# Rolling a large matrix by DMA: the long row pieces copied in 16 DMAs of whole pieces, or in 512 DMAs of half pieces

## The chip, the cores and the metric

One core of a Trainium2 chip runs the kernel; the other cores do nothing. The metric is the device time of one execution in microseconds (us). The kernel before took 818.08 us, the median of 11 runs that lie between 815.44 and 820.29 us.

## What is computed

The reference is a circular shift of every row:

```
x = np.random.randn(8192, 8192).astype(np.float32)
shift = 100
return np.roll(x, shift, axis=1)
```

Nothing is calculated. Each output row is the input row moved 100 columns to the right, and the last 100 columns of the input come first. 268.44 MB are read from the chip's memory and 268.44 MB are written to it.

## The kernel before

The kernel splits every output row in two at column a = 128, the shift rounded up to a multiple of 128 columns (512 bytes). The long piece, columns 128 to 8191 (32,256 bytes), is copied from memory to memory without touching the on-chip memory. The short head, columns 0 to 127 (512 bytes), takes another way. The source of the long piece begins at column g = 28, which is byte 112 of the row.

**The long pieces** (lines 30 to 37). A row number is written as 64c + 4e + j, with c from 0 to 127, e from 0 to 15 and j from 0 to 3. The views `xm` and `om` (lines 30 and 31) put j first, then e, then c. Line 37 issues one DMA for each of 4 blocks of c and each of 4 values of j: 16 DMAs. The outermost dimension of a DMA is e with 16 values, so that each of the core's 16 DMA engines gets the rows of one e; within a DMA an engine has `depth` = 32 rows, one for each c of the block. One DMA moves 16 x 32 rows, 16,128 KB. An even j goes to the queue of SyncE (SP) and an odd j to that of ScalarE (ACT):

```
engines[j % 2].dma_start(out=om[j, :, cs, a:], in_=xm[j, :, cs, g:n_cols - s])
```

So each of the two queues issues 8 DMAs. In the profile the DMA ring that SP feeds is q1 and the one that ACT feeds is q10. SP and ACT do nothing else in this kernel.

**The heads** (lines 54 to 76). GpSimd (POOL) issues them on a queue of its own (ring q0): in two stages k it reads the pieces for 4096 rows each into on-chip tiles `t` and `h` (lines 67, 68 and 71), VectorE copies parts of `t` into `h` (lines 69 and 72), and at the end POOL issues 8 DMAs that write `h` to the output (line 76). The heads are 8.39 MB of the traffic on the rings. Nothing on SP or ACT depends on them.

**What sets the order.** The program is written in a framework that places the waits itself. It gives each DMA a completion semaphore out of a small set and uses them in turn. The trace shows eight of them on SP and ACT, four on each queue. The fifth DMA of a queue therefore waits until the first one has landed on all 16 engines, the sixth waits for the second, and so on: at most four DMAs of a queue are in flight. No DMA of the long pieces waits for anything else.

Of the kernel before, what the change touches and what calls it, by code (L numbers as in the profile page):

```python
# [1 line left out]

# [4 lines left out]


@with_exitstack
def kernel(  # L10
    ctx: ExitStack,
    tc: tile.TileContext,
    x: bass.AP,
    shift: int,
    out: bass.AP,
):
    nc = tc.nc
    n_rows, n_cols = x.shape
    s = shift % n_cols
    a = -(-s // 128) * 128  # L20
    g = a - s
    P = nc.NUM_PARTITIONS
    engines = [nc.sync, nc.scalar]
    n_chunks = 16
    rows = n_rows // n_chunks

    xm = x.rearrange("(c e j) w -> j e c w", e=16, j=4)  # L30
    om = out.rearrange("(c e j) w -> j e c w", e=16, j=4)
    depth = n_rows // 64 // 4
    for c in range(4):
        for j in range(4):
            if a < n_cols:
                cs = slice(c * depth, (c + 1) * depth)
                engines[j % 2].dma_start(out=om[j, :, cs, a:], in_=xm[j, :, cs, g:n_cols - s])
    if a == 0:
        return


    if a > 512:
        for i in range(n_chunks):
            r = slice(i * rows, (i + 1) * rows)
            nc.gpsimd.dma_start(out=out[r, :s], in_=x[r, n_cols - s:])
            if g > 0:
                nc.gpsimd.dma_start(out=out[r, s:a], in_=x[r, :g])
        return

    Q, J = 4, 8
    n_st = n_rows // (P * Q * J)
    reads = ctx.enter_context(tc.tile_pool(name="reads", bufs=n_st))
    heads = ctx.enter_context(tc.tile_pool(name="heads", bufs=n_st))
    xt = x.rearrange("(k p j q) c -> k q p j c", q=Q, j=J, p=P)
    ot = out.rearrange("(k p j q) c -> k q p j c", q=Q, j=J, p=P)
    tiles = []  # L60
    for k in range(n_st):
        t = reads.tile([P, Q - 1, J, a], x.dtype)
        h = heads.tile([P, Q, J, a], x.dtype)
        for q in range(1, Q):
            lead = bass.AP(tensor=x.tensor, offset=(k * P * J * Q + q) * n_cols - s,
                           ap=[[J * Q * n_cols, P], [Q * n_cols, J], [1, a]])
            nc.gpsimd.dma_start(out=t[:, q - 1], in_=lead)  # L67
        nc.gpsimd.dma_start(out=h[:, Q - 1, :, :s], in_=xt[k, Q - 1, :, :, n_cols - s:])  # L68
        nc.vector.tensor_copy(h[:, :Q - 1, :, :s], t[:, :, :, :s])  # L69
        if g > 0:  # L70
            nc.gpsimd.dma_start(out=h[:, 0, :, s:], in_=xt[k, 0, :, :, :g])  # L71
            nc.vector.tensor_copy(h[:, 1:, :, s:], t[:, :, :, s:])  # L72
        tiles.append(h)
    for k, h in enumerate(tiles):
        for q in range(Q):
            nc.gpsimd.dma_start(out=ot[k, q, :, :, :a], in_=h[:, q])  # L76


# [1 line left out]
_INS = ['x', 'shift']  # L80
_OUTS = [((8192, 8192), 'float32')]

_NUMBERS = {'shift': 100}


# [26 lines left out]
```

## Time and profile before

| | us |
|---|---|
| median of 11 runs | 818.08 |
| lowest and highest | 815.44 and 820.29 |
| the profiled execution's own time | 817.92 |
| its span, first to last instruction | 816.1 |
| VectorE busy | 3.7 |
| GpSimd busy | 16.1 |
| issue to landing, long pieces, median, SP and ACT | 399.4 and 398.3 |

The span is what the profile's views cover; the other 1.8 us of the profiled execution lie around it. A "packet" in the profile is one contiguous run of bytes that one DMA engine moves, or the 4-byte write with which that engine reports the end of its part of a DMA. The "share of 16 engines" of a ring is the time its packets took, divided by 16 engines times the span. "GB/s" counts each byte once, as it passes through a DMA engine; a copy from memory to memory loads the memory twice for it, once as a read and once as a write.

### The profile page before, as it was taken

What the parts mean: (1) busy time and instruction counts of PE and PEld (TensorE: products, weight loads), DVE (VectorE), ACT (ScalarE), POOL (GpSimd) and SP (SyncE); (2) the same over time, 40 slices, a digit from 0 to 9 for tenths busy, and PEclk for the clock granted to TensorE, in tenths of its full rate; (3) what the DMA queues carried; (4) which work ended last, traced back from release to release, by engine and by line L of the source; (5) the groups of instructions that cost most, each with busy time, mean ns of one, the idle gap of its engine ahead of it and who ended that gap; (6) DMA issues with size and microseconds to landing.
All of it is one profiled execution on the core that took longest, in us unless ns stands there. A gap on an engine that the chain in (4) does not pass through costs nothing. (4 is left out here: it accounts for less than half of the span.)

```text
span 816.1 us, 93 instructions
## 1 busy us (share of the span) xinstructions
DVE 3.7 (0%) x4; POOL 16.1 (2%) x22
## 2 busy tenths in 40 slices
DVE  0000000000000000000000000000000000000000
POOL 3000001000010000000000000000000000000000
DMA  9999999999999999999999999999999999999996
GB/s 305 329 338 339 339 341 333 340 337 338 342 336 341 340 339 351 336 347 342 349 336 341 346 327 332 330 341 338 334 327 337 329 337 332 330 330 334 338 332 250
DMA packets 10784, 272.63 MB, mean 334 GB/s; under 512 B 544, under 2 KB 544, under 8 KB 2592
## 3 DMA queue, kind: packets, MB, share of 16 engines
q10 hardware_dynamic: 4224, 132.12, 47.4%
q1 hardware_dynamic: 4224, 132.12, 46.7%
q0 software_dynamic: 2336, 8.39, 4.6%
HBM read 268.44 MB, written 268.44 MB: 658 GB/s over the span
## 5 line engine op out<-in xcount | busy, mean ns | idle before, releaser
L76 POOL DMA_DIRECT2D out_dram<-h x8 | 6.9, 956 | 171.0 <-DMA h<-in_x_dram 145.3
L67 POOL DMA_DIRECT2D t<-in_x_dram x6 | 5.4, 910 | 0.8 <-PEq L107 0.8
L69 DVE COPY h<-t 128x2400 f32<-128x2400 f32 x2 | 2.8, 1410 | 209.2 <-DMA t<-in_x_dram 209.2
L71 POOL DMA_DIRECT2D h<-in_x_dram x2 | 1.8, 882 | 28.4 <-DMA t<-in_x_dram 28.4
L68 POOL DMA_DIRECT2D h<-in_x_dram x2 | 1.8, 882 | 27.6 <-DMA t<-in_x_dram 27.6
L72 DVE COPY h<-t 128x672 f32<-128x672 f32 x2 | 1.0, 502 | 0.0
L93 POOL MEMSET const-float32-0.0<- 128x1 f32 x1 | 0.1, 98 | 0.2 <-issue 0.2
L93 POOL MEMSET const-bfloat16-1.0<- 128x1 bf16 x1 | 0.1, 102 | 0.0
L93 POOL MEMSET const-float32-1.0<- 128x1 f32 x1 | 0.1, 100 | 0.0
L93 POOL MEMSET const-uint8-127<- 128x1 uint8 x1 | 0.1, 99 | 0.0
## 6 DMA issues: line engine op xcount, KB each, us to landing
out_dram<-in_x_dram SPq DMA_DIRECT2D x8, 16128.0 KB, 399.4
out_dram<-in_x_dram ACTq DMA_DIRECT2D x8, 16128.0 KB, 398.3
out_dram<-h POOLq DMA_DIRECT2D x8, 512.0 KB, 183.9
t<-in_x_dram POOLq DMA_DIRECT2D x6, 512.0 KB, 118.7
h<-in_x_dram POOLq DMA_DIRECT2D x2, 400.0 KB, 151.9
h<-in_x_dram POOLq DMA_DIRECT2D x2, 112.0 KB, 146.8
```

What stands on the lines that cost most here:

```text
L67: nc.gpsimd.dma_start(out=t[:, q - 1], in_=lead)
L68: nc.gpsimd.dma_start(out=h[:, Q - 1, :, :s], in_=xt[k, Q - 1, :, :, n_cols - s:])
L69: nc.vector.tensor_copy(h[:, :Q - 1, :, :s], t[:, :, :, :s])
L71: nc.gpsimd.dma_start(out=h[:, 0, :, s:], in_=xt[k, 0, :, :, :g])
L72: nc.vector.tensor_copy(h[:, 1:, :, s:], t[:, :, :, s:])
L76: nc.gpsimd.dma_start(out=ot[k, q, :, :, :a], in_=h[:, q])
L93: nc = _bacc.Bacc("TRN2", target_bir_lowering=False, num_devices=1)
```

## The change

Each long piece is cut in two at column `mid`. With a = 128 and 8192 columns, mid = (128 + 8192) // 2 rounded down to a multiple of 128, which is 4096. The left half is columns 128 to 4095 (15,872 bytes) and goes to SP; the right half is columns 4096 to 8191 (16,384 bytes) and goes to ACT. The loop over c now takes two values of c at a time, 64 blocks in place of 4, so that a DMA holds two half rows for each of the 16 engines: 16 x 2 pieces, 496 KB on SP and 512 KB on ACT. There are 64 x 4 x 2 = 512 DMAs, 256 on each queue, where there were 16. The heads are not touched.

```
     xm = x.rearrange("(c e j) w -> j e c w", e=16, j=4)
     om = out.rearrange("(c e j) w -> j e c w", e=16, j=4)
-    depth = n_rows // 64 // 4
-    for c in range(4):
+    mid = (a + n_cols) // 2 // 128 * 128
+    for c in range(0, n_rows // 64, 2):
         for j in range(4):
-            if a < n_cols:
-                cs = slice(c * depth, (c + 1) * depth)
-                engines[j % 2].dma_start(out=om[j, :, cs, a:], in_=xm[j, :, cs, g:n_cols - s])
+            for q, (lo, hi) in enumerate(((a, mid), (mid, n_cols))):
+                if lo < hi:
+                    engines[q].dma_start(out=om[j, :, c:c + 2, lo:hi], in_=xm[j, :, c:c + 2, lo - s:hi - s])
```

## The prediction, made before the changed kernel was run

> **What bounds the kernel now.** I read the DMA part of the page first, since no compute engine is busy for more than 2% of the span. The columns of the ring lines are packets, MB, and the share of 16 engines' time.
>
> ```profile
> DMA packets 10784, 272.63 MB, mean 334 GB/s; under 512 B 544, under 2 KB 544, under 8 KB 2592
> ## 3 DMA queue, kind: packets, MB, share of 16 engines
> q10 hardware_dynamic: 4224, 132.12, 47.4%
> q1 hardware_dynamic: 4224, 132.12, 46.7%
> q0 software_dynamic: 2336, 8.39, 4.6%
> HBM read 268.44 MB, written 268.44 MB: 658 GB/s over the span
> ```
>
> The three rings fill 98.7% of the engines' time, so the transfers are the bound. The next question decides most of this forecast: is it the engines, or the memory behind them? The DMA view in two windows tells, 100 to 200 us, where the heads are under way, and then 500 to 600 us, where they are done.
>
> ```profile
> q10 hardware_dynamic: 511, 16.00, 45.5%
> q1 hardware_dynamic: 510, 15.93, 43.4%
> q0 software_dynamic: 512, 1.82, 10.7%
> ```
>
> ```profile
> q1 hardware_dynamic: 529, 16.55, 49.8%
> q10 hardware_dynamic: 533, 16.68, 49.7%
> ```
>
> A long-piece byte loads the memory twice, a head byte once (its other side is on chip). Early: 2 x 31.93 + 1.82 = 65.7 MB in 100 us. Late: 2 x 33.23 = 66.5 MB. The heads took 10.7% of the engines' time and carried 2.8% of the memory traffic, so 7.9% of engine time was poorly used, and the traffic was only 1.2% lower: a ratio of 0.15. The table of windows says the same of the end (columns: busy engines, clock, DMA share, GB/s).
>
> ```profile
> 700.00:780.00 80.00, 0.00 (x0) 0.00 (x0) 1.00 1.00 333
> 786.00:801.00 15.00, 0.00 (x0) 0.00 (x0) 1.00 0.94 329
> 801.00:807.00 6.00, 0.00 (x0) 0.00 (x0) 1.00 0.88 328
> 807.00:816.10 9.10, 0.00 (x0) 0.00 (x0) 1.00 0.38 156
> ```
>
> With 12% of the engine time idle the rate falls from 333 to 328, by 1.5%: a ratio of 0.13. So up to about 12% of lost engine time costs some 0.14 of itself. The memory is the bound, the engines are nearly so.
>
> Last, the waits on SP's queue, and the landing times.
>
> ```profile
> SPq L107 <- DMA out_dram<-in_x_dram: 316.0, 4, 99.6
> SPq L37 <- DMA out_dram<-in_x_dram: 48.5, 4, 17.1
> ```
>
> ```profile
> out_dram<-in_x_dram SPq DMA_DIRECT2D x8, 16128.0 KB, 399.4
> out_dram<-in_x_dram ACTq DMA_DIRECT2D x8, 16128.0 KB, 398.3
> ```
>
> Four waits at L37 for eight DMAs: numbers 5 to 8 each wait for the semaphore of the DMA four places earlier. Four in flight at some 100 us each give the 399 us to landing. These waits cost nothing now, since hundreds of microseconds of work stand on the rings.
>
> **What the Trainium skill says.** "DMA: Bandwidth & Descriptors", section "Issuing engines are not separate DMA queues": DMAs from SP, ACT and POOL run on the same 16 engines and interleave. The trace agrees: in its packet records, chained end to start, a 32,256-byte packet of one ring is followed by one of the other ring in all but 17 of some 5,000 pairs. "HBM Reference", section "Specifications (TRN2)": about 716 GB/s for the memory of a core pair. The 658 GB/s here are 92% of that, which fits a memory bound. "DMA: Bandwidth & Descriptors", section "How a descriptor splits into AXI transactions": a piece that doesn't start on a 256-byte boundary also fetches the bytes below its start. No view here shows that; I use it below.
>
> **The change part by part.** The sum is made against the profiled execution, 817.92 us (span 816.1), which stands 0.16 us below the median of 818.08.
>
> *More packets.* An engine has 8192 / 16 = 512 rows. Before: 512 data packets and 16 completion packets. After: 1,024 data packets and 512 completion packets (one for each of 512 DMAs), so 512 + 496 more. A completion packet lasts 9 ns in the records. The shortest 32,256-byte packet took 1,192 ns and the shortest 4,096-byte one 159 ns: 0.0367 ns a byte and 9 ns fixed. So 1,008 x 9 ns = 9.1 us of engine time, 1.1%. At the ratio 0.14 that is +1.3 us; the bounds are 0 (wholly hidden) and +9.1 (nothing hidden).
>
> *More boundaries between DMAs.* Does a completion packet hold up what follows? In the records the data packet after one lasted 1,399 ns against 1,505 usual (60 cases before 465 us), and 1,585 against 1,547 (90 cases after). The sign changes, so I take 0. The upper bound is 496 x 38 ns = 19 us of engine time, +2.6 us at 0.14; the lower bound is 0, since a boundary can free nothing.
>
> *The split read.* The right half's source starts at byte 3,996 x 4 = 15,984, which is 62 x 256 + 112. By the section named, 112 more bytes are fetched for each row, against 64,512 read and written: 0.17%, +1.4 us as an estimate at full memory price. If whole transactions count, it is one more on about 253, +3.2 us. If the memory serves the same bytes again at no cost, 0. I take +0.7, between 0 and 1.4, because the neighbour half is fetched at about the same time.
>
> *More instructions.* SP and ACT each issue 256 DMAs in place of 8. Unhindered issues in this trace last 0.61 to 0.67 us on SP and 0.67 to 0.90 on ACT: 256 x 0.9 = 230 us at most on a queue that has 816. SP and ACT have no other work, so nothing stands behind a waiting issue but the next one. Cost 0. The cover is the work already on the rings, next item.
>
> *The window of four.* Each DMA now waits for the one four places earlier, so a ring holds at most 4 x 2 data packets for each engine, and both rings 16 packets at about 1.55 / 2 = 0.77 us: 12.4 us of work where it was some 400. Refilling takes 0.4 us from the completion packet to the landing (107.3 to 107.7 in the trace) and about 1.4 us from an issue to the first packet (0.74 to 2.18 at the start, when 512 pieces were prepared; now 32): about 2 us, perhaps 4 under load. The slowest engine always has work. An engine that leads by more than some 7 to 10 us goes idle. The completion packets show the leads: of the last DMA, one engine ends at 786.0 us, two at 803.2 and 803.7, the other thirteen from 808.2 to 814.8. Three engines are held back, the pack is not. Idle time of three engines for part of the run stays below the 12% that the memory covers: 0. It becomes a cost in the rival below.
>
> *The end.* What the uneven end can cost: after 807 us 1.42 MB take 7.8 us up to 814.8, where 333 GB/s would need 4.3; with 0.3 us from the stretches before it, 3.8 us are at stake. The window cuts the lead of one engine from 29 to some 8 us, but the spread of the other engines, 6.6 us, is within the window and stays. I take -1.0; bounds -3.8 and 0.
>
> *The start.* SP's first packets begin at 2.18 us, ACT's at 5.40, but all engines are busy from 2.18 on. A smaller first DMA may start sooner: bounds -0.7 and 0. I take 0.
>
> *POOL's ring.* The heads now take turns with packets half as long, so they end earlier than the 465 us of now. Nobody waits for them before the end of the program. Their bytes are the same: 0, and 350 us of room if that is wrong.
>
> Sum: +1.3 + 0.7 - 1.0 = +1.0. 817.92 + 1.0 = 818.9, and 819.1 on the median; I say 819.0.
>
> **The rivals.**
>
> A, the forecast: the memory stays the bound and the small terms nearly cancel, 819.0. Its own range is 816 to 822: the small terms near zero beside a larger gain at the end give 816, and the boundaries or the transactions at their upper ones 821 to 822. Chance 0.52.
>
> B, slower: *the window of four runs dry.* The place is the wait for the slowest of 16 engines in every DMA, 3.1 us apart on each queue. If the refill takes 5 us and not 2, an engine whose lead is above some 6 us is idle in each turn. Half of the engines idle for 2 us of every 12.4 is 8% of engine time; at 0.14 that is 1.1%, +9 us: 828. It decides from the point at which idle time passes 12%, a DMA share below about 0.88 in the middle of the run: there the cover is gone, and each further per cent costs a whole one. For it: waits that had hundreds of microseconds of work behind them now have 12, and a refill under load isn't shown by this trace. Against it: 12.4 us are three to six times the refill. Chance 0.27.
>
> C, faster: *the window evens the engines out.* If holding the leaders gives the late engines their share of the memory, all end within 2 us. -3.8 at the end and -0.7 at the start, the packet terms hidden: 813.4. For it: one engine is 29 us early at the end, and this is the memory's share moved from late engines to an early one. Against: most of the 3.8 us comes from the pack's own 6.6 us. Chance 0.20.
>
> D: the framework sees the small rectangles as overlapping and chains all DMAs. 512 x (1.55 + about 2 us) = 1.8 ms. Against it: the interleaved rows of before, and the split at column 128 between heads and long pieces, got no such wait. Chance 0.01.
>
> **How the numbers follow.** About 0.2% (1.6 us) is what a measurement of this kernel can tell from no change. A falls within 0.2% with 0.35, above with 0.11, below with 0.06. With B and D (0.28) slower is 0.39; with C (0.20) faster is 0.26; same 0.35. The range 812 to 830 holds A, C and B at their prices, and the packets at their full price (827); it leaves out D and the worst of B and C.
>
> **What would show it.** q1 and q10 with 12,288 packets each, 130.0 and 134.2 MB; 8,480 packets under 512 B. SP's waits at L37 for nearly the whole span in 252 pieces, issue to landing near 12 us. Right if the windows in the middle still show 332 to 334 GB/s late, with a DMA share from 0.95 up; B if the share drops under 0.92 and the rate with it; C if all engines' last completions lie within 3 us. Wrong in another way if the share stays full and the rate differs by over 1%: then the memory itself answers differently to half pieces or to engines in closer step.

## The result, and the profile after

The changed kernel takes 823.07 us (median of 12 runs, 821.82 to 823.96); the kernel before took 818.45 us in the runs beside it (47 runs, 815.44 to 820.70). The ratio is 1.0056, with a 95% interval of 1.0045 to 1.0067. The change makes the kernel slower by 0.56%, 4.6 us. The profiled execution has a span of 822.0 us where it was 816.1.

The DMA part of the page of the changed kernel (columns of the ring lines: packets, MB, share of 16 engines):

```profile
DMA packets 26916, 272.70 MB, mean 332 GB/s; under 512 B 8480, under 2 KB 8480, under 8 KB 10528
## 3 DMA queue, kind: packets, MB, share of 16 engines
q10 hardware_dynamic: 12288, 134.23, 48.2%
q1 hardware_dynamic: 12288, 130.04, 47.1%
q0 software_dynamic: 2336, 8.39, 4.1%
...
HBM read 268.44 MB, written 268.44 MB: 653 GB/s over the span
```

The packets are those that were counted ahead: 12,288 on each ring, 8,480 of the short kind. The engines are more fully used than before, 99.4% against 98.7%, and yet they moved the same bytes in more time. The landing times on the same page, and the waits on SP's queue:

```profile
out_dram<-in_x_dram ACTq DMA_DIRECT2D x256, 512.0 KB, 12.5
out_dram<-in_x_dram SPq DMA_DIRECT2D x256, 496.0 KB, 12.7
```

```profile
SPq L39 <- DMA out_dram<-in_x_dram: 644.9, 239, 7.7
SPq L109 <- DMA out_dram<-in_x_dram: 18.8, 8, 8.0
```

A DMA is in flight for 12.5 us, as foreseen. SP waits for 645 us of the span at L39, in 239 pieces; nearly the whole span in 252 pieces had been foreseen. (Its 256 DMA instructions take 571 ns each at the median, 146 us together.) The waits are long and cost nothing in themselves, as the windows of the changed kernel show (columns: the stretch and its length, busy time of VectorE and GpSimd, clock, DMA share, GB/s):

```profile
500.00:600.00 100.00, 0.00 (x0) 0.00 (x0) 1.00 1.00 332
600.00:700.00 100.00, 0.00 (x0) 0.00 (x0) 1.00 1.00 330
786.00:801.00 15.00, 0.00 (x0) 0.00 (x0) 1.00 0.99 330
807.00:816.00 9.00, 0.00 (x0) 0.00 (x0) 1.00 0.99 334
816.00:822.00 6.00, 0.00 (x0) 0.00 (x0) 1.00 0.43 153
```

The same stretches of the middle in the kernel before:

```profile
500.00:600.00 100.00, 0.00 (x0) 0.00 (x0) 1.00 0.99 332
600.00:700.00 100.00, 0.00 (x0) 0.00 (x0) 1.00 1.00 334
```

The DMA share is 1.00 in the middle after the change, so no engine runs dry. The end is better than before: the full rate lasts until 816 us, 6 us before the end of the span; before it was 807 us, 9 us before the end. The last completions of SP's ring lie between 807.3 and 812.1 us, those of ACT's between 818.3 and 820.8 (packet records of the trace); the engine that was 29 us early is gone. The loss is in the middle, where the rate is 330 to 332 GB/s against 332 to 334, and in the first 100 us, where the heads pass. The rings in these 100 us, before and then after the change:

```profile
q1 hardware_dynamic: 500, 16.10, 43.2%
q10 hardware_dynamic: 473, 15.22, 42.3%
q0 software_dynamic: 468, 1.73, 12.7%
```

```profile
q10 hardware_dynamic: 1316, 14.49, 38.2%
q1 hardware_dynamic: 1309, 13.92, 36.5%
q0 software_dynamic: 1281, 4.58, 23.4%
```

Counted as memory traffic (twice the long pieces, once the heads) they moved 61.4 MB against 64.4. Which of the two stretches holds the cost of the change, the traces of these two kernels alone can't tell.

A small account puts it together. Engine time in use is the sum of the ring shares times the span; the rest of the span is unused. From the packet records, in us for the mean engine:

| | span | long-piece data packets | completion packets | heads' packets | unused |
|---|---|---|---|---|---|
| before | 816.1 | 767.8 | 0.1 | 37.2 | 11.0 |
| after | 822.0 | 778.3 | 4.6 | 34.1 | 5.0 |

The changed kernel gains 6.0 us of unused time and 3.1 us at the heads, and pays 10.5 us in longer data packets and 4.5 us in completions: 5.9 us between these two executions, 4.6 us in the medians. The table says where the time stands, not what caused it.

### The profile page after: what moved, and what is told of

It is laid out like the page before. It is cut to its first block, busy times and chain, and to the rows that moved or that the text cites. A ratio compares the mean times of both kernels' runs of the same rounds, so it can differ in the third digit from the quotient of the medians.

```text
span 822.0 us, 589 instructions
## 1 busy us (share of the span) xinstructions
DVE 3.7 (0%) x4; POOL 16.0 (2%) x22
## 2 busy tenths in 40 slices
DMA packets 26916, 272.70 MB, mean 332 GB/s; under 512 B 8480, under 2 KB 8480, under 8 KB 10528
## 3 DMA queue, kind: packets, MB, share of 16 engines
q10 hardware_dynamic: 12288, 134.23, 48.2%
q1 hardware_dynamic: 12288, 130.04, 47.1%
## 6 DMA issues: line engine op xcount, KB each, us to landing
out_dram<-in_x_dram ACTq DMA_DIRECT2D x256, 512.0 KB, 12.5
out_dram<-in_x_dram SPq DMA_DIRECT2D x256, 496.0 KB, 12.7
```

## The experiments

The kernel before took 832 to 833 us on the chips that ran the experiments, so every run is given as a ratio, with its 95% interval, to the kernel before on its own chip. The ratio can differ by some 0.2% from the quotient of the two medians. Four kernels ran together on each of three chips.

### First set: one part alone, and both kernels without the heads

In the first 100 us the heads' ring took 23.4% of the engine time after the change and 12.7% before. The lines above show why: the three rings move nearly equal numbers of packets there, 468 beside 473 and 500 before, 1,281 beside 1,309 and 1,316 after, so more and shorter packets on the long-piece rings mean more turns for the heads' ring. The first theory was that this is the loss (T), against the window of four (W).

Half pieces in DMAs of 32 rows, against the changed kernel:

```diff
-    for c in range(0, n_rows // 64, 2):
+    for c in range(0, n_rows // 64, 32):
...
-                    engines[q].dma_start(out=om[j, :, c:c + 2, lo:hi], in_=xm[j, :, c:c + 2, lo - s:hi - s])
+                    engines[q].dma_start(out=om[j, :, c:c + 32, lo:hi], in_=xm[j, :, c:c + 32, lo - s:hi - s])
```

Whole pieces in DMAs of two rows, against the kernel before:

```diff
-    depth = n_rows // 64 // 4
-    for c in range(4):
+    depth = n_rows // 64 // 64
+    for c in range(64):
```

No heads, in both kernels:

```diff
-    if a == 0:
-        return
+    return
```

Half pieces, 32 rows:

> Half pieces by ring as in the change, but in DMAs of 32 rows per engine, 16 on each queue. Theory T (packet length): the heads' ring gets a turn after every half-length packet, so its share of engine time between 20 and 100 us is about 25% as after the change (12.6% before), and the 3.9 us that the change lost there come back; the steady part is slower by 1 to 2 us. So 822 to 824 us, 0.4 to 0.7% slower than before. Rival W (window): the loss comes from the many small DMAs with four in flight, which are undone here, so 818 to 819 us, no difference.

Measured: 835.38 us (832.01 to 844.25), 1.0044 (1.0026 to 1.0062).

Whole pieces, two rows:

> Whole pieces by the parity of j as before, but in DMAs of two rows per engine, 128 on each queue. T: packets are as long as before, so the heads' share between 20 and 100 us stays near 12.6% and nothing is lost there; 240 more completion packets per engine cost under 1 us, the end gains 1 to 2 us: 816 to 818.5 us. W: small DMAs with four in flight are what costs, so 821 to 823 us.

Measured: 839.12 us (836.59 to 842.36), 1.0090 (1.0065 to 1.0115).

Before, no heads:

> The kernel before without the heads: columns 0 to 127 of the output are not written. 528.5 MB of memory traffic at the 666 GB/s of the late part are 793.5 us, with about 7 us at both ends: 800 us.

Measured: 812.63 us (811.16 to 813.76), 0.9770 (0.9748 to 0.9791).

After, no heads:

> The changed kernel without the heads: columns 0 to 127 of the output are not written. T: without the heads' ring the 3.9 us of the first 100 us are not lost; what is left is the steady rate, 0.5% lower, against a better end: 1 to 2 us above the kernel before without heads (801 to 802 us). W: the small DMAs cost the same with or without heads: 4 to 5 us above it (804 to 805 us).

Measured: 817.02 us (816.06 to 817.62), 0.9820 (0.9797 to 0.9843).

T fails. Without any heads the changed kernel is still 4.4 us slower (817.02 - 812.63), as much as with them; and whole pieces in small DMAs, where T expected no loss, lost most. The heads cost 19.5 us in the kernel before (832.1 - 812.63). T's figure for the half pieces in long DMAs came true (1.0044), but not its reason: the heads' ring took 18.0% of the engine time between 20 and 100 us there, and about 25% had been expected. W isn't borne out either. Its 4 to 5 us for the kernels without heads came true, but the half pieces alone, in long DMAs, lose 0.44% where it expected nothing. Each part alone costs something, and together they cost no more than one of them, so the parts don't add up. The rings' shares of the two kernels without heads, before and after in this order:

```profile
span 811.7 us, 61 instructions
...
q1 hardware_dynamic: 4224, 132.12, 49.5%
q10 hardware_dynamic: 4224, 132.12, 49.2%
```

```profile
span 815.8 us, 557 instructions
...
q10 hardware_dynamic: 12288, 134.23, 49.9%
q1 hardware_dynamic: 12288, 130.04, 49.2%
```

98.7% of 811.7 are 801.2 us in use and 10.5 unused; 99.1% of 815.8 are 808.5 in use and 7.3 unused. The engines need 7.3 us more for the same bytes, and 3.2 us less are unused, 3.1 of them in the last 30 us: the end is more even. That is the result with the heads taken out of it.

### Second set: is it the completions, or the window?

The same DMAs without the heads, issued without the framework and so without its waits: one semaphore for each queue, waited for at the end only. The lines below are the half pieces beside those of the changed kernel (`sh` is its `s`); the two kernels of whole pieces are written in the same way. Theory C below (completions) is not the rival C of the prediction.

```diff
-                    engines[q].dma_start(out=om[j, :, c:c + 2, lo:hi], in_=xm[j, :, c:c + 2, lo - s:hi - s])
+                    eng.dma_start(out=om[j, :, c:c + 2, lo:hi], in_=xm[j, :, c:c + 2, lo - sh:hi - sh]).then_inc(sem, 16)
+                    n += 16
+            eng.wait_ge(sem, n)
```

Half pieces, two rows, no window:

> The changed kernel's 512 DMAs without the heads (columns 0 to 127 of the output are not written), with one semaphore for each queue that is waited for only at the end: no window of four, the same packets. Theory C (completions): 512 completion packets per engine cost engine time in full, 9 ns each and perhaps more, window or not, so about the time of the changed kernel without heads, 0.5% or more above the kernel of 32-row DMAs without a window. Theory H (held leaders): the window makes all engines keep the pace of the slowest; without it the leaders run ahead again, and the time is within 0.2% of the kernel of 32-row DMAs without a window.

Measured: 829.26 us (822.38 to 831.23), 0.9957 (0.9935 to 0.9979).

Whole pieces, two rows, no window:

> Whole pieces by the parity of j in DMAs of two rows per engine, without heads (columns 0 to 127 of the output are not written) and without the window of four: 256 completion packets per engine, as in the run with whole pieces and the window, which was 0.9% slower than before. C: the packets after a completion are 38 ns longer there, so the loss stays without the window: about 1% above the kernel of 32-row DMAs. H: the loss goes with the window, within 0.2% of it.

Measured: 817.26 us (816.66 to 818.34), 0.9820 (0.9803 to 0.9838).

Whole pieces, 32 rows, no window:

> The kernel before without the heads (columns 0 to 127 of the output are not written), one semaphore per queue waited for at the end. The base for the two other kernels without a window. The wait for the DMA four places earlier never held a ring up before, so both theories expect the time of the kernel before without heads, 0.977 of the kernel before.

Measured: 813.75 us (810.85 to 816.36), 0.9774 (0.9752 to 0.9795).

The changed kernel without heads, again:

> The changed kernel without the heads once more (columns 0 to 127 of the output are not written), with its window of four, to stand beside the kernels without one: 0.982 of the kernel before. C: the same as the half pieces without a window. H: 0.5% above them.

Measured: 817.07 us (816.88 to 817.88), 0.9819 (0.9802 to 0.9836).

H fails clearly, and so does the rival B of the prediction: taking the window away doesn't bring the half pieces back to the time of the long DMAs, it makes them 1.4% slower than with it. The window of four helps them. That it is the window and not the framework, whole pieces in 32-row DMAs show: 0.9774 without the framework, 0.9770 with it. The profiled execution was the fastest of that kernel's ten, so its page shows the least of it. Its landing times and rings:

```profile
span 820.6 us, 541 instructions
...
q10 hardware_dynamic: 12288, 134.23, 49.6%
q1 hardware_dynamic: 12288, 130.04, 48.7%
...
out_dram<-in_x_dram ACTq DMA_DIRECT2D x256, 512.0 KB, 78.1
```

With the window of four gone a DMA is in flight for 78 us. It isn't gone without limit: the DMA instructions of a queue now last 3.0 us at the median, where they lasted 0.57, so the issuing itself is held back, at an estimated 24 DMAs in flight on each queue (78.1 us to landing, one DMA in 820.6 / 256 = 3.2 us). The time in use is 98.3% of 820.6, 806.7 us, no more than with the window (808.5 and, in the repeat, 99.1% of 815.1 = 807.8), but 13.9 us are unused in place of 7.3. C is only half right here: the time in use stays up without the window, as it said, but the total isn't the one it gave.

Whole pieces in two-row DMAs stand 3.5 us above those in 32-row DMAs without a window (817.26 and 813.75), 0.4%: more than H's 0.2% and less than half of C's 1%. Their rings:

```profile
span 816.5 us, 285 instructions
...
q1 hardware_dynamic: 6144, 132.13, 49.3%
q10 hardware_dynamic: 6144, 132.13, 49.2%
```

98.5% of 816.5 are 804.3 us in use, where the whole pieces in 32-row DMAs have 799.3 (98.8% of 809.0) and 801.2. So smaller DMAs of the same data packets stand with 3 to 5 us more time in use. Their 240 further completions for each engine are 2.2 us of that.

### Third set: more packets, more completions, fewer completions, even rings

Theory F says that every further packet costs its 9 ns in full, M that the memory hides most of it.

Quarter pieces in DMAs of 32 rows, against the half pieces in DMAs of 32 rows, with the heads taken out as above:

```diff
-            for q, (lo, hi) in enumerate(((a, mid), (mid, n_cols))):
+            for q, (lo, hi) in enumerate(((a, 2048), (2048, mid), (mid, 6144), (6144, n_cols))):
...
-                    engines[q].dma_start(out=om[j, :, c:c + 32, lo:hi], in_=xm[j, :, c:c + 32, lo - s:hi - s])
+                    engines[q % 2].dma_start(out=om[j, :, c:c + 32, lo:hi], in_=xm[j, :, c:c + 32, lo - s:hi - s])
```

One half row, against the changed kernel, again without heads (eight half rows: 8 and `c + 8` in the same places, with the heads):

```diff
-    for c in range(0, n_rows // 64, 2):
+    for c in range(0, n_rows // 64, 1):
...
-                    engines[q].dma_start(out=om[j, :, c:c + 2, lo:hi], in_=xm[j, :, c:c + 2, lo - s:hi - s])
+                    engines[q].dma_start(out=om[j, :, c:c + 1, lo:hi], in_=xm[j, :, c:c + 1, lo - s:hi - s])
```

Even rings, against the changed kernel:

```diff
-                    engines[q].dma_start(out=om[j, :, c:c + 2, lo:hi], in_=xm[j, :, c:c + 2, lo - s:hi - s])
+                    engines[(q + j) % 2].dma_start(out=om[j, :, c:c + 2, lo:hi], in_=xm[j, :, c:c + 2, lo - s:hi - s])
```

Quarter pieces:

> Quarter pieces (7,680 and 8,192 bytes) in DMAs of 32 rows per engine, two quarters on each ring, without heads (columns 0 to 127 of the output are not written): 2,048 data packets per engine in place of 512, and only 64 completions. Theory F (full price): the 9 ns of every further packet are paid, 1,536 x 9 = 13.8 us above the kernel before without heads (0.977 of before): 0.993 to 0.995. Theory M (the forecast's: the memory hides all but 0.14 of lost engine time): 2 us, 0.979 to 0.980.

Measured: 856.84 us (847.95 to 860.52), 1.0268 (1.0223 to 1.0313).

One half row:

> The changed kernel with one half row per engine and DMA, without heads (columns 0 to 127 of the output are not written): 1,024 completions per engine in place of 512, the same data packets, and a window of four DMAs that is only some 6 us long. F: 512 x 9 = 4.6 us above the changed kernel without heads (0.982 of before): 0.986 to 0.989. M: 0.7 us, 0.982 to 0.983. Rival B of the forecast (the window runs dry): clearly above 0.99, with engine time unused in the middle of the run.

Measured: 814.98 us (812.96 to 815.31), 0.9778 (0.9751 to 0.9805).

Eight half rows:

> The changed kernel, heads included, with eight half rows per engine and DMA: 128 completions per engine in place of 512, the same data packets, a window of some 50 us. F: 3.5 us less for completions, but the leaders are no longer held and the end is as uneven as before, so 1.002 to 1.006 of before. M: 1.000 to 1.002.

Measured: 841.45 us (833.99 to 844.68), 1.0089 (1.0059 to 1.0120).

Even rings:

> The changed kernel, heads included, with the halves exchanged between the rings for odd j, so that both rings carry the same bytes. In the changed kernel SP's ring ended 8.7 us before ACT's. If the last stretch on one ring costs anything, up to 2 us are gained: 1.003 to 1.005 of before. If not, it is the time of the changed kernel, 1.0056.

Measured: 834.60 us (832.15 to 836.66), 1.0024 (1.0012 to 1.0036).

F fails. Twice the completions make the kernel not slower but, within the intervals, as fast as the kernel before without heads (0.9778 beside 0.9770). A quarter of the completions gains nothing. Quarter pieces lose 5% against the kernel before without heads, some 41 us (1.0268 less 0.9770, of 832.7), of which 9 ns a packet explain 14. M fails at the same three. B is refuted a second time: the shortest window of all, 6.3 us to landing, leaves no engine dry, as the page of the kernel with one half row shows, with its rings at 99.4% of the engine time.

```profile
span 813.4 us, 1069 instructions
...
q10 hardware_dynamic: 16384, 134.25, 50.4%
q1 hardware_dynamic: 16384, 130.06, 49.0%
...
out_dram<-in_x_dram ACTq DMA_DIRECT2D x512, 256.0 KB, 6.3
```

In use are 99.4% of 813.4, 808.5 us, the same as in the changed kernel without heads, though the completions take 9.2 us and not 4.6 (their data packets are 4.2 us shorter); unused are 4.9 in place of 7.3. The quarter pieces lose in another place. The window 200 to 780 us of their trace, and that of the kernel before without heads:

```profile
200.00:780.00 580.00, 0.00 (x0) 1.00 0.95 319
```

```profile
200.00:780.00 580.00, 0.00 (x0) 1.00 1.00 328
```

5% of the engine time is unused in the middle of the run there, the rate is 2.7% lower, and their last completions are spread from 806.8 to 845.0 us. Why their engines are not fed in the middle was not tried, nor were quarter pieces in small DMAs.

The two kernels with heads, eight half rows and then even rings, ran on one chip. Their spans and rings:

```profile
span 841.9 us, 205 instructions
...
q10 hardware_dynamic: 9216, 134.22, 47.4%
q1 hardware_dynamic: 9216, 130.03, 46.4%
q0 software_dynamic: 2336, 8.39, 4.3%
```

```profile
span 833.7 us, 589 instructions
...
q10 hardware_dynamic: 12288, 132.14, 47.7%
q1 hardware_dynamic: 12288, 132.14, 47.3%
q0 software_dynamic: 2336, 8.39, 4.1%
```

In use are 98.1% of 841.9 and 99.1% of 833.7: 825.9 and 826.2 us, the same. The 8 us between them are all unused time, 16.0 against 7.5. The half pieces in 32-row DMAs, from the first set:

```profile
span 837.9 us, 109 instructions
...
q10 hardware_dynamic: 8448, 134.22, 47.5%
q1 hardware_dynamic: 8448, 130.02, 46.2%
q0 software_dynamic: 2336, 8.39, 3.9%
```

97.6% of 837.9 are in use and 20.1 us unused. The traces show what goes with this. Each of the 16 engines reports the end of its part of a DMA, and the time from the first report to the last is how far the engines stand apart (median of all DMAs of a kernel; the kernels without a window have one semaphore for all DMAs of a queue and don't show it):

| pieces, rows per DMA | issue to landing, ACT, us | first to last engine, us | unused, us |
|---|---|---|---|
| half, 1 (no heads) | 6.3 | 1.6 | 4.9 |
| half, 2, changed kernel | 12.5 | 5.6 | 5.0 |
| half, 2, no heads (two runs) | 12.6 and 12.5 | 5.9 and 5.5 | 7.3 and 7.3 |
| half, 2, even rings | 12.7 | 5.8 | 7.5 |
| half, 8 | 51.2 | 25.4 | 16.0 |
| half, 2, no window, no heads | 78.1 | | 13.9 |
| half, 32 | 202.9 | 43.4 | 20.1 |
| quarter, 32, no heads | 102.7 | 53.5 | 62.6 |
| whole, 2 | 26.0 | 14.3 | 10.9 |
| whole, 32, kernel before | 398.3 | 25.2 | 11.0 |
| whole, 32, no heads | 402.2 | 27.8 | 10.5 |

Short windows keep the engines together, and half pieces need that more than whole ones. In DMAs of 32 rows the engines stand 25 to 28 us apart with whole pieces, 43 with half and 54 with quarter pieces. Whole pieces leave 9.7 to 11.0 us unused with some 400 us to landing, and no less with 26. Among the long windows of half pieces the order isn't shown: the execution without a window was the fastest of its ten, those of 8 and 32 rows are among the slower ones of their kernels (843.96 and 839.70 us, medians 841.45 and 835.38). Even rings measured 1.0024 where the changed kernel has 1.0056. As that was another chip, and as the two kernels were not run side by side with heads, a gain from even rings is likely but not shown. The unused time is no smaller (7.5 us against 5.0, on two chips), so nothing points to the end as its place.

None of the twelve kernels is faster than the kernel before with the same work.

## Why the prediction was right and wrong

The result lies inside the range of 812 to 830, and slower was the likeliest of the three signs (0.39). It isn't the likeliest case: A's own range ended at 822, and 823.07 lies beyond it. B had the sign and not the mechanism. Of the signs that A named, the DMA share came true and the rate didn't: 330 to 332 GB/s in the middle, not 332 to 334. That the sum still came within 4.1 us of the result (819.0) is in part luck, as two of its terms were too small in opposite directions.

*The bound.* Right in that the engines stay full (DMA share 1.00). Wrong was the sentence that decided the forecast, "up to about 12% of lost engine time costs some 0.14 of itself". It came from the stretch with heads and from the uneven end, and was used for packets of another kind. Even for idle engines it isn't a rule: the quarter pieces leave 5% of the engine time unused in the middle and lose 2.7% of the rate (319 against 328 GB/s), a ratio near one half. In the kernels without heads 9.1 us of counted packet time came back as 7.3 us of engine time in use, and the repeat on another chip gives 8.5 (807.8 against the 799.3 of whole pieces without a window): 0.8 to 0.9 of the count. That is no price of a packet either: with twice the completions the time in use didn't grow.

*More packets, +1.3 us, and the split read, +0.7.* This is the term that was mis-sized: 2.0 us together where 7.3 were measured without heads. The upper bound given, +9.1 with "nothing hidden", is nearer in number, but its mechanism, the full price for each packet, is theory F, which failed. In the account of the two kernels without heads completions are 4.5 of the 7.3 us and longer data packets 2.5, which is where the time stands and not what caused it: with one half row the completions take 9.2 us and the data packets 4.2 less. What raised the time in use stays open. The split read was not tried alone, so what the Trainium skill ("DMA: Bandwidth & Descriptors", section "How a descriptor splits into AXI transactions") says of reads that don't start on a 256-byte boundary is neither borne out nor refuted here.

*More boundaries, 0.* Not settled. Twice as many boundaries cost nothing with one half row, but whole pieces, with 240 more boundaries for each engine and the same data packets, lost 0.4% without window and heads and 0.9% with both.

*More instructions, 0.* Right. SP waited for 645 us at L39, so issuing is far from the bound; the median issue is 571 ns on SP and 578 on ACT.

*The window of four, 0.* Right for the idle time, and 12.5 us to landing is the 12.4 that was worked out. But it was priced only as a danger. It is a gain, seen without heads: without it the half pieces are 1.4% slower.

*The end, -1.0 us.* Right in sign, too small: 3.2 us less are unused without heads. In the changed kernel it is 6.0, of which 3.6 lie behind 786 us, by the DMA shares of the windows (7.3 us unused there before, 3.7 after), close to the -3.8 that was given as the bound. The prediction let the pack's spread of 6.6 us stay; in the changed kernel the last completions on ACT's ring, which ended last, lie within 2.5 us. Rival C's mechanism is real, and the sign that was asked for it (within 3 us) is there. It was outweighed.

*The start and POOL's ring, 0.* The heads' ring did take 23.4% of the engine time in the first 100 us, which the prediction didn't put in figures; the first packet starts at 2.20 us, as before (2.18). In the sum no cost is seen: the heads cost 19.5 us in the kernel before, and the changed kernel with heads stands 2.4% above the one without (1.0056 less 0.9820), 19.6 us of 832; with the intervals of the ratios and the different chips, some 2 us either way can't be told apart. The heads are done by 180 us in place of 465.

Measured against the sum: +7.3 us of time in use, where +2.0 had been put for packets and reading, and -3.2 us unused, where -1.0 had been put for the end. That makes +4.1 without heads in the two profiled executions, 4.4 in the medians, and 4.6 with heads.

*What stays open.* What raises the time in use. Why two-row DMAs of whole pieces lose 0.4 to 0.9%, with packets no shorter than before; why quarter pieces leave engines without work in the middle; and why one half row per DMA takes up its completions where two don't. One rival stands untried: the order of the rows. With the size of a DMA the order changes too, since `c` is the outer loop and `j` the inner one. On each engine a ring before took 32 rows that lie 64 rows apart and then went on to another j; now it does so after two of them. The two rings were on different rows and are now on the two halves of the same rows. Every kernel with another DMA size has another order, and no run changed one without the other. The trace has no addresses and no view of the memory's side, so it can't tell them apart.

## What to carry to other kernels

When a copy has its DMA engines full, count the engine time of every added packet and completion, and keep both ends, nothing and the full price, in the range. A discount that was measured on one kind of lost engine time doesn't carry over to another: here the same count came back nearly in full, not at all, and three times over (half pieces in two-row DMAs, one half row, quarter pieces in long DMAs). Then write down separately the time in use and the time unused: a change like this one moves both, in opposite directions. With long DMAs short pieces let the engines drift apart here, and little work in flight held them together; a window of a few DMAs that looks like a danger may be what keeps the end even.

## What the runs showed of the hardware that was not expected

The 16 engines drift apart under equal loads: in the kernel before, the last of them ends its part of a DMA 25 us after the first (median), in the kernel with one half row 1.6 us.

The rings don't stay in step when each waits for its own DMAs: SP's ring, with 3% fewer bytes, ended 8.7 us ahead of ACT's in the changed kernel (812.1 and 820.8 us), and 13.7 us ahead with one half row (798.6 and 812.3). Without the window both ended at the same 819.6 us.

A DMA of 1/4 MB with only four of them in flight on each queue kept the engines at 99.4%. So a small DMA didn't leave the engines idle here. Quarter pieces of about 8 KB in DMAs of 4 MB did: the engines ran at 0.95 in the middle and the copy took 5% longer. Whether the short piece alone does that, or only together with the long DMA, was not tried.

The same kernel before takes 818 us on one chip and 832 on others, a difference three times that of the change.
